# FFN's plain product with the weights stationary and all 512 tokens moving

## The chip, the cores and the metric

One core of a Trainium2 chip runs the whole program. The metric is the device time of one execution in microseconds. The engines are named as the profile names them: PE multiplies matrices (PEld loads its stationary operand), DVE and ACT are the vector and the scalar engine, POOL and SP issue most transfers.

## The reference

```python
def swiglu(x, w_in, w_out):
    gu = x @ w_in
    g, u = jnp.split(gu, 2, axis=-1)
    return (jax.nn.silu(g) * u) @ w_out
...
    for l in range(DEPTH):
        x = x + 0.5 * swiglu(rms_norm(x, ffn1_norm[l]), ffn1_w_in[l], ffn1_w_out[l])
        x = x + mixer(...)
        x = x + 0.5 * swiglu(rms_norm(x, ffn2_norm[l]), ffn2_w_in[l], ffn2_w_out[l])
    return rms_norm(x, final_norm)
```

There are 512 tokens of 1024 features, an inner width of 2816 and two layers, so four FFNs in all, all in float32. The change lies in the FFNs alone.

## The kernel before, in words

Every float32 product is made of three passes over halves of the operands: high times high, high times low, low times high. ACT writes the high half of a weight granule (`whi`, L201), DVE the low one (`wlo`, L208), out of `raw` granules of 512 KB that SP loads and to some of which POOL adds a second granule in flight. `ws.next()` hands out the next granule with two more already split; `raw` has nine buffers, `whi` and `wlo` three each.

An FFN (`stage_ffn`) first makes the 256 gate and the 256 up columns that are left over from its recursive scheme: this is the plain product `cl`. The other 5 × 512 columns follow in blocks `jb` = 0 to 4, each of seven products of Strassen's kind, called A, B, C in the trace. PSUM has eight banks of 128 × 512: the plain product holds four of them, A two, B two, and C, where it occurs, two more.

The input of the FFN lies transposed, features on the partitions: `xh` and `xl` are its high and low halves, in quarters of 4 × 128 features by 256 tokens. The first FFN gets them from a transposed copy of x. For the three later ones the last one or two quarters are transposed on PE while the plain product is already running (`norm.settle`, L670).

Before, a plain matmul has 128 tokens stationary and the 512 columns of the weights (256 gate, 256 up) moving, so the result has the tokens on its partitions. `plain(kt, w, kk, js)` does one feature tile `kt` for token halves `js`; features 4 to 7 are done for token half 1 first and then for half 0. `plain_out` applies 1/rms, which in this layout is one number per partition (`norm.r`, 128 × 4), in Silu's scale on ACT (L739) and in a multiply on DVE (L741). The outcome `th` must have the features on its partitions for the output product, so `late_at` and `to_at` (L643) send it through PE: eight 128 × 128 transposes for each FFN, and ACT copies the result to `at` (L647).

Engines run their own queues in order. DVE's and ACT's order is mostly that of a scheduler; PE's order follows the code.

Of the kernel before, what the change touches and what calls it, by code (L numbers as in the profile page):

```python
# [9 lines left out]
F32 = mybir.dt.float32  # L10
# [88 lines left out]
def encoder_kernel(  # L99
# [29 lines left out]
    def bank(s="ps"):  # L129
        return pp.tile([P, T], F32, tag="ps", name=nm(s))  # L130

    def pair(s="ps"):
        return [bank(s), bank(s)]
# [241 lines left out]
    def run(terms, again=False, late=False):  # L375

        if late:
            for ps, lh, ll, rh, rl, w, start, stop in terms:
                PE.matmul(ps, lh, rh, start=start, stop=False)
            for ps, lh, ll, rh, rl, w, start, stop in terms:  # L380
                PE.matmul(ps, ll, rh, start=False, stop=False)
            for ps, lh, ll, rh, rl, w, start, stop in terms:
                PE.matmul(ps, lh, rl, start=False, stop=stop)
            return
        for ps, lh, ll, rh, rl, w, start, stop in terms:
            PE.matmul(ps, lh, rh, start=start, stop=False, skip_group_check=again)  # L386
            PE.matmul(ps, *((lh, rl) if w == "l" else (ll, rh)), start=False, stop=False, skip_group_check=again)  # L387
        for ps, lh, ll, rh, rl, w, start, stop in terms:
            PE.matmul(ps, *((ll, rh) if w == "l" else (lh, rl)), start=False, stop=stop, skip_group_check=again)  # L389
# [227 lines left out]
    def snap(ps):  # L617
        t = slot(F32, "sn", (2, T))
        for b in range(2):
            S.activation(t[:, b, :], ps[b], AF.Copy)  # L620
        return t
# [5 lines left out]
    def stage_ffn(norm, nxt, late):  # L627
# [4 lines left out]
        def at_tile(h, j, c):  # L632
            if (h, j, c) not in at:
                at[h, j, c] = slot(F32, "at")
            return at[h, j, c]
# [14 lines left out]
                        S.activation(at_tile(h, j, c)[:, i, :], tr[:, k, :], AF.Copy)  # L650


        pcl = [pair("cl"), pair("cl")]

        def plain(kt, w, kk, js):
            wh, wl = w
            c = slice(kk * T, (kk + 1) * T)
            i, k = divmod(kt, 4)
            terms = []
            for j in js:  # L660
                for b in range(2):
                    t = slice((2 * j + b) * P, (2 * j + b + 1) * P)
                    terms.append((pcl[j][b], hx[i][:, k, t], lx[i][:, k, t], wh[:, c], wl[:, c], "r", kt == 0, kt == DT - 1))
            run(terms, late=not (norm.idx or kt))

        for g in range(2):
            w = ws.next()
            for kk in range(2):
                plain(2 * g + kk, w, kk, (0, 1))
            norm.settle()  # L670

        raw = norm.raw
        b11, b12, b21, b22 = raw[0, 0], raw[0, 1], raw[1, 0], raw[1, 1]

        w2 = [ws.next(), ws.next()]
        for js in ((1,), (0,)):
            for g in range(2):
                for kk in range(2):
                    plain(4 + 2 * g + kk, w2[g], kk, js)
        first = norm.idx == 0  # L680
        if not first:
            norm.rstd()
# [48 lines left out]
            5: t1, 6: t2, 7: t3,  # L731
        }
        late_at = []
        def plain_out():
            for j in range(2):
                th = slot(F32, "th", (2, 256))
                for b in range(2):
                    c = 2 * j + b
                    S.activation(th[:, b, :], pcl[j][b][:, 0:256], AF.Silu, scale=norm.r[:, c : c + 1])  # L739
                    u = pcl[j][b][:, 256:512]  # L740
                    V.scalar_tensor_tensor(th[:, b, :], u, norm.r[:, c : c + 1], th[:, b, :], ALU.mult, ALU.mult)  # L741
                late_at.append((th, j, 0, 2))

        if norm.idx:
            plain_out()

        def settle_at():
            while late_at:
                to_at(*late_at.pop(0))
# [73 lines left out]
        def pair_block(jb, late_at):  # L823

            one = jb in PAIRS
            pa = pair("A")
            product(pa, acts[1], K4, True)
            s1 = snap(pa)
            settle_at()
            if one:  # L830
                qa = kept["a"] = bank("qA")
                inner(qa, 1, True)
                V.tensor_tensor(s1[:, 0, :], qa, s1[:, 0, :], ALU.add)
            pb = pair("B")
            product(pb, acts[5], K4, True)
            sb = snap(pb)
            qa = kept["a"]
            if one:
                qb = bank("qB")
                inner(qb, 5, True)  # L840
                tb = kept["s"] = slot(F32, "sq", (2, T))[:, 0, :]
                S.activation(tb, qb, AF.Copy)
            else:
                tb = kept["s"]
                inner(qa, 7, False)
                V.tensor_tensor(tb, qa, tb, ALU.subtract)
                V.tensor_tensor(s1[:, 1, :], tb, s1[:, 1, :], ALU.subtract)
            settle_at()
            product(pa, acts[6], K4, False, again=True)
            s2 = snap(pa)  # L850
            if one:
                qc = bank("qC")
                inner(qc, 2, True)
                V.tensor_tensor(s1[:, 0, :], qc, s1[:, 0, :], ALU.subtract)
            else:
                inner(qa, 4, False)
                V.tensor_tensor(s1[:, 0, :], qa, s1[:, 0, :], ALU.subtract)
                z1 = gate(s1, 0)
            product(pa, acts[7], K4, False, again=True)
            less(pa, sb)  # L860
            if one:
                inner(qa, 6, False)
                V.tensor_tensor(s1[:, 1, :], qa, s1[:, 1, :], ALU.add)
            product(pb, acts[3], K4, False, again=True)
            less(pb, s2)
            z2 = gate(s2, 1)
            times(z2, [sb[:, 0, :], sb[:, 1, :]], 1)
            if one:
                inner(qb, 3, False)
                V.tensor_tensor(s1[:, 1, :], qb, s1[:, 1, :], ALU.subtract)  # L870
                z1 = gate(s1, 0)
            if jb == NB - 1:
                make(0)
                make(1)
            product(pa, acts[4], K4, False, again=True)
            times(z1, pa, 0)
            late_at += [(z2, 1, 2 + 4 * jb, 4), (z1, 0, 2 + 4 * jb, 4)]

        for jb in range(NB):
            f0 = 2 + 4 * jb  # L880
            if jb:
                if jb == 1:
                    inner_split()
                pair_block(jb, late_at)
                continue
            if first and jb == 0:
                with tc.manual_schedule(engines={mybir.EngineType.DVE, mybir.EngineType.Activation}):
                    pa = pair("A")
                    product(pa, acts[1], K4, True)
                    for j in range(2):  # L890
                        t = snap(pcl[j])
                        pcl[j] = [t[:, 0, :], t[:, 1, :]]
                    s1 = snap(pa)
                    second(s1)
                    pb = pair("B")
                    product(pb, acts[5], K4, True)
                    sb = snap(pb)
                    norm.squares(1, 1)
                    product(pa, acts[6], K4, False, again=True, ahead=1)
                    s2 = snap(pa)  # L900
                    for _ in norm.roots(0, 4):
                        pass
                    plain_out()
            else:
                pa, pb, s1, sb = two(jb)
                settle_at()
                product(pa, acts[6], K4, False, again=True)
                s2 = snap(pa)
            settle_at()
            if jb or not first:  # L910
                second(s1)
            z1 = gate(s1, 0)
            product(pa, acts[7], K4, False, again=True)
            less(pa, sb)
            product(pb, acts[3], K4, False, again=True)
            less(pb, s2)
            z2 = gate(s2, 1)
            times(z2, [sb[:, 0, :], sb[:, 1, :]], 1)
            if jb == NB - 1:
                make(0)  # L920
                make(1)
            product(pa, acts[4], K4, False, again=True)
            times(z1, pa, 0)
            late_at += [(z2, 1, f0, 4), (z1, 0, f0, 4)]
# [1220 lines left out]
```

## Time and profile before

| | |
|---|---|
| median of 3 runs | 1859.5 us (1858.61 to 1860.37) |
| profiled execution | 1858.22 us, span of its trace 1856.4 us |
| busy, of the span | PE 100%, PEld 85%, DVE 84%, ACT 65%, POOL 11% |
| chain that ended last | PE 99% |
| granted PE clock | 0.999 |
| transposes of FFN results (L643) | 352 in all, 32 of them for the plain products |

The span runs from the first to the last instruction of the trace; the 1.8 us beside it lie outside of it. A row of the timeline gives start, duration, engine, line, operation, result<-operands, shapes and count; for a matmul the moving operand comes first and the stationary one second. Ends of matmuls are modelled, their starts are recorded, so distances between starts are what counts on PE.

### The profile page before, as it was taken

Reading aid. Unit: us, or ns where it says so; the run is one execution under the profiler, and the core shown is the slowest. Engines: PE = TensorE matmul, PEld = TensorE weight load, DVE = VectorE, ACT = ScalarE, POOL = GpSimd, SP = SyncE. Lnnn points to the kernel's source line nnn. Section 1 sums busy time; section 2 is a strip of 40 time slices with the busy share of each in tenths; the row PEclk is TensorE's granted clock in tenths of the full one; section 3 lists DMA queues with packets and bytes.
Section 4 is the critical chain, followed back from the end, with each engine's and each line's share of the span. In section 5 each row is a group of like instructions: output and inputs, shape, how many; then the busy total and the mean of one; then the engine's idle time right before and its main releaser. Section 6 shows DMA issues by size and latency. Waiting matters only on the chain.

```text
span 1856.4 us, 26124 instructions
## 1 busy us (share of the span) xinstructions
PE 1847.7 (100%) x9564; PEld 1575.1 (85%) x9564; DVE 1556.3 (84%) x1915; ACT 1201.9 (65%) x1787; POOL 196.3 (11%) x235
## 2 busy tenths in 40 slices
PE   9999999999999999999999999999999999999998
PEld 7888888889998888888888888888899988888886
DVE  8888899758879787889978788997687797878898
ACT  6766666758656656666666666667676576656665
POOL 0011010100211011101001110110002100110010
PEclk9999999999999999999999999999999999999999
DMA  9788788774998479869757986987649984788695
GB/s 302 227 246 227 222 238 268 250 190 133 252 248 229 132 210 256 230 203 263 241 145 210 253 226 205 254 270 243 203 131 256 238 230 128 221 243 242 197 276 181
DMA packets 118385, 413.94 MB, mean 223 GB/s; under 512 B 13409, under 2 KB 13537, under 8 KB 118257
## 3 DMA queue, kind: packets, MB, share of 16 engines
q1 hardware_dynamic: 85712, 297.78, 45.6%
q0 software_dynamic: 32112, 113.71, 32.6%
q8 instruction: 75, 1.23, 0.3%
q10 hardware_dynamic: 432, 0.79, 0.1%
q14 instruction: 54, 0.43, 0.1%
HBM read 404.49 MB, written 6.29 MB: 221 GB/s over the span
## 4 chain that ended last, share of the span: by engine, by line
PE 99%; DVE 1%; issue 0%; ACT 0%; DVEq 0%; ACTq 0%
PE A L386 9%; PE A L389 9%; PE A L387 9%; PE o L386 7%; PE o L389 7%; PE o L387 7%; PE B L386 5%; PE B L387 5%; PE B L389 5%; PE ps L386 3%; PE ps L387 3%; PE ps L389 3%; PE tr L643 2%; PE cl L387 2%; PE cl L389 2%; PE cl L386 2%
## 5 line engine op out<-in xcount | busy, mean ns | idle before, releaser
L208 DVE TENSOR_TENSOR wlo<-raw,whi 128x1024 fp32r<-128x1024 f32 (+1 forms) x540 | 638.9, 1192 | 169.9 <-ACT whi L201 169.0
L201 ACT ACTIVATE whi<-raw 128x1024 fp32r<-128x1024 f32 (+1 forms) x540 | 555.1, 1033 | 318.8 <-PE A L387 89.7
L160 POOL DMA_DIRECT2D raw<-in_wst_dram x186 | 160.9, 869 | 1457.0 <-DMA raw<-in_wst_dram 755.9
L194 DVE TENSOR_TENSOR raw<-raw,raw 128x1024 f32<-128x1024 f32 (+1 forms) x144 | 171.3, 1194 | 2.7
L386 PE MATMUL A<-whi,xh 128*128 128x512 f32 x320 | 124.5, 389 | 0.0
L387 PE MATMUL A<-whi,xl 128*128 128x512 f32 x320 | 124.5, 389 | 0.0
L199 ACT ACTIVATE whi<-raw 128x1024 fp32r<-128x1024 f32 x84 | 87.2, 1038 | 42.1 <-issue 21.5
L206 DVE SCALAR_TENSOR_TENSOR wlo<-raw,whi 128x1024 fp32r<-128x1024 f32 x84 | 99.7, 1196 | 4.6 <-ACT whi L199 4.5
L389 PE MATMUL A<-wlo,xh 128*128 128x512 f32 x320 | 92.1, 389 | 0.0
L620 ACT ACTIVATE sn<-A 128x512 f32<-128x512 f32 x96 | 56.2, 591 | 46.4 <-PE A L389 46.3
L755 ACT ACTIVATE th<-sn,r 128x512 f32<-128x512 f32 x80 | 56.1, 715 | 46.2 <-DVE sn L625 42.5
L389 PEld LDWEIGHTS A<-wlo,xh 128*128 128x128 f32 x320 | 60.1, 188 | 12.5
L387 PEld LDWEIGHTS A<-whi,xl 128*128 128x128 f32 x320 | 60.1, 188 | 12.5
L386 PEld LDWEIGHTS A<-whi,xh 128*128 128x128 f32 x320 | 60.1, 188 | 12.4
L386 PE MATMUL B<-whi,t1h 128*128 128x512 f32 x160 | 63.0, 394 | 0.0
L386 PE MATMUL A<-whi,t2h 128*128 128x512 f32 x160 | 62.5, 391 | 0.0
L387 PE MATMUL B<-whi,xl 128*128 128x512 f32 x160 | 62.3, 390 | 0.0
L387 PE MATMUL B<-whi,t1l 128*128 128x512 f32 x160 | 62.3, 389 | 0.0
L387 PE MATMUL A<-whi,t2l 128*128 128x512 f32 x160 | 62.3, 389 | 0.0
L386 PE MATMUL A<-whi,t3h 128*128 128x512 f32 x160 | 62.3, 389 | 0.0
L387 PE MATMUL A<-whi,t3l 128*128 128x512 f32 x160 | 62.2, 389 | 0.0
L386 PE MATMUL B<-whi,xh 128*128 128x512 f32 x160 | 62.2, 389 | 0.0
(498 smaller groups left out, 4910.9 us busy)
## 6 DMA issues: line engine op xcount, KB each, us to landing
raw<-in_wst_dram SPq DMA_DIRECT2D x503, 512.0 KB
raw<-in_wst_dram POOLq DMA_DIRECT2D x200, 512.0 KB, 8.2
raw<-in_wst_dram SPq DMA_DIRECT2D x28, 256.0 KB
vc<-vd SPq DMA_DIRECT2D x28, 256.0 KB
bm<-in_near_dram SPq DMA_DIRECT2D x16, 384.0 KB
vd<-v SPq DMA_DIRECT2D x8, 512.0 KB
dft<-in_dft_dram POOLq DMA_DIRECT2D x4, 514.0 KB, 9.3
x<-in_xin_dram SPq DMA_DIRECT2D x4, 512.0 KB
```

Of the source, the lines that this page charges most:

```text
L160: z = G.dma_start(out=self.t, in_=wst[GRAN_AT[plus]][:, 0 : self.n], accum_op=ALU.add)
L194: V.tensor_tensor(self.raw.t, self.raw.t, self.add.t, ALU.add)
L199: S.activation(self.out[0][:, cs], self.raw.t[:, cs], AF.Copy, scale=-1.0)
L201: S.activation(self.out[0][:, cs], self.raw.t[:, cs], AF.Copy)
L206: self.last = V.scalar_tensor_tensor(lo, t, -1.0, hi.bitcast(F32), ALU.mult, ALU.subtract)
L208: self.last = V.tensor_tensor(lo, t, hi.bitcast(F32), ALU.subtract)
L386: PE.matmul(ps, lh, rh, start=start, stop=False, skip_group_check=again)
L387: PE.matmul(ps, *((lh, rl) if w == "l" else (ll, rh)), start=False, stop=False, skip_group_check=again)
L389: PE.matmul(ps, *((ll, rh) if w == "l" else (lh, rl)), start=False, stop=stop, skip_group_check=again)
L620: S.activation(t[:, b, :], ps[b], AF.Copy)
L643: PE.transpose(tr[:, k, b * P : (b + 1) * P], a[:, b, (q + k) * P : (q + k + 1) * P], ident)
L755: S.activation(th[:, b, :], g[:, b, :], AF.Silu, scale=norm.r[:, c : c + 1])
```

## The change

The plain product changes sides: 128 columns of the weights are stationary and all 512 tokens move. Banks `cl` 0 and 1 hold the gate features, 2 and 3 the up features, with features on the partitions. The count of matmuls stays (12 for each of 8 feature tiles). 1/rms now varies along the free dimension and has to be the same on all partitions: `spread_root` writes the 128 × 4 numbers to DRAM, four bytes apiece, and reads the 512 of them back to each of the 128 partitions (256 KB into `rr`), both on SP's queue. `plain_out` multiplies by `rr` on DVE, takes Silu on ACT and writes the product straight into `at`. It no longer stands right behind the plain product: in the three later FFNs it comes after the third product of block 0 (A, second time), in the first FFN in block 2.

```diff
-        pcl = [pair("cl"), pair("cl")]
-        def plain(kt, w, kk, js):
+        pcl = [bank("cl") for _ in range(4)]
+        def plain(kt, w, kk):
...
-            for j in js:
-                for b in range(2):
-                    t = slice((2 * j + b) * P, (2 * j + b + 1) * P)
-                    terms.append((pcl[j][b], hx[i][:, k, t], lx[i][:, k, t], wh[:, c], wl[:, c], "r", kt == 0, kt == DT - 1))
-            run(terms, late=not (norm.idx or kt))
+            mh, ml = hx[i][:, k, :], lx[i][:, k, :]
+            cs = [slice(kk * T + cb * P, kk * T + cb * P + P) for cb in range(4)]
+            if not norm.idx:
+                order = ((wh, mh), (wh, ml), (wl, mh))
+            else:
+                order = ((wh, mh), (wl, mh), (wh, ml))
...
+            for n, (lh, rh) in enumerate(order):
+                for cb in range(4):
+                    PE.matmul(
+                        pcl[cb], lh[:, cs[cb]], rh, start=first and n == 0 and len(order) == 3,
+                        stop=last and n == len(order) - 1,
+                    )
...
-        w2 = [ws.next(), ws.next()]
-        for js in ((1,), (0,)):
-            for g in range(2):
-                for kk in range(2):
-                    plain(4 + 2 * g + kk, w2[g], kk, js)
+        for g in range(2):
+            w = ws.next()
+            for kk in range(2):
+                plain(4 + 2 * g + kk, w, kk)
...
+        def spread_root():
+            rd = dp.tile([TB, P], F32, tag="rd", name=nm("rd"))
+            spread["r"] = t = slot(F32, "rr", (2, T))[:, 0, :]
+            nc.sync.dma_start(out=bass.AP(tensor=rd.tensor, offset=rd.offset, ap=[[1, P], [P, TB]]), in_=norm.r)
+            nc.sync.dma_start(out=t, in_=bass.AP(tensor=rd.tensor, offset=rd.offset, ap=[[0, P], [1, T]]))
...
-                    S.activation(th[:, b, :], pcl[j][b][:, 0:256], AF.Silu, scale=norm.r[:, c : c + 1])
-                    u = pcl[j][b][:, 256:512]
-                    V.scalar_tensor_tensor(th[:, b, :], u, norm.r[:, c : c + 1], th[:, b, :], ALU.mult, ALU.mult)
-                late_at.append((th, j, 0, 2))
+            r = spread.pop("r")
+            for f in range(2):
+                t = slot(F32, "th", (2, T))
+                V.tensor_tensor(t[:, 0, :], pcl[f], r, ALU.mult)
+                S.activation(t[:, 0, :], t[:, 0, :], AF.Silu)
+                V.tensor_tensor(t[:, 1, :], pcl[2 + f], r, ALU.mult)
+                for j in range(2):
+                    c = slice(j * 256, (j + 1) * 256)
+                    V.tensor_tensor(at_tile(0, j, 0)[:, f, :], t[:, 0, c], t[:, 1, c], ALU.mult)
         if norm.idx:
-            plain_out()
+            spread_root()
...
+            if first and jb == 2:
+                plain_out()
...
-            if jb or not first:
+            if not first:
+                plain_out()
                 second(s1)
```

In the first FFN ACT still copies the four banks to two tiles `sn` at once, before and after, so its banks come free early.

Three places of the built order follow. The first is PE in the second FFN of the first layer, block 0, where product B ends and the second use of A begins; before:

```order
2838 L389 MATMUL B_6197<-wlo_6177,t1h_6123 128x512 x2
2839 L643 MATMUL tr_6236<-ident,th_6145 128x128 x4
2840 L643 MATMUL tr_6243<-ident,th_6150 128x128 x4
2841 L386 MATMUL A_6155<-whi_6198,t2h_6133 128x512
2842 L387 MATMUL A_6155<-whi_6198,t2l_6134 128x512
```

and the same place in the changed kernel:

```order
2831 L387 MATMUL B_6185<-whi_6164,t1l_6118 128x512
2832 L389 MATMUL B_6185<-wlo_6165,t1h_6117 128x512 x2
2833 L386 MATMUL A_6143<-whi_6186,t2h_6127 128x512
2834 L387 MATMUL A_6143<-whi_6186,t2l_6128 128x512
2835 L386 MATMUL A_6143<-whi_6186,t2h_6127 128x512
```

The eight transposes are gone and A follows on B. The second place is DVE in the same block, around product C, in the changed kernel (`cl_5947` to `cl_5950` are the banks of the plain product in order, `C_6277` and `C_6278` those of C):

```order
677 L208 TENSOR_TENSOR wlo_6227<-raw_6015,whi_6226 128x1024
678 L208 TENSOR_TENSOR wlo_6245<-raw_6045,whi_6244 128x1024
679 L756 TENSOR_TENSOR th_6263<-cl_5947,rr_6140 128x512
680 L758 TENSOR_TENSOR th_6263<-cl_5949,rr_6140 128x512
681 L761 TENSOR_TENSOR at_6267<-th_6263 128x256
682 L761 TENSOR_TENSOR at_6269<-th_6263 128x256
683 L756 TENSOR_TENSOR th_6271<-cl_5948,rr_6140 128x512
684 L758 TENSOR_TENSOR th_6271<-cl_5950,rr_6140 128x512
685 L208 TENSOR_TENSOR wlo_6282<-raw_6075,whi_6281 128x1024
686 L761 TENSOR_TENSOR at_6267<-th_6271 128x256
687 L761 TENSOR_TENSOR at_6269<-th_6271 128x256
688 L208 TENSOR_TENSOR wlo_6300<-raw_6145,whi_6299 128x1024
```

Before, the rows 679 to 684, 686 and 687 are not here; four multiplies of 128 × 256 (L741) stand instead about ten rows earlier, next to the first granules of block 0. C's first bank is the one that row 679 reads and its second the one that row 680 reads. The third place is SP's queue at the beginning of the same FFN, in the changed kernel:

```order
205 L158 DMA raw_6145<-in_wst_dram 128x1024
206 L749 DMA rd_6139<-r_6107 128x4x1
207 L158 DMA raw_6203<-in_wst_dram 128x1024
208 L750 DMA rr_6140<-rd_6139 128x512
209 L158 DMA raw_6224<-in_wst_dram 128x1024
```

Rows 206 and 208 are new; the loads around them keep their order. Row 208 waits for row 206 to land, and the loads from row 209 on stand behind it.

More of the change, by code (lines that the diff above doesn't have):

```diff
@@ L650, in to_at @@
                         S.activation(at_tile(h, j, c)[:, i, :], tr[:, k, :], AF.Copy)
-        pcl = [pair("cl"), pair("cl")]
-        def plain(kt, w, kk, js):
+        pcl = [bank("cl") for _ in range(4)]
+        def plain(kt, w, kk):
             wh, wl = w
-            c = slice(kk * T, (kk + 1) * T)
             i, k = divmod(kt, 4)
-            terms = []
-            for j in js:
-                for b in range(2):
-                    t = slice((2 * j + b) * P, (2 * j + b + 1) * P)
-                    terms.append((pcl[j][b], hx[i][:, k, t], lx[i][:, k, t], wh[:, c], wl[:, c], "r", kt == 0, kt == DT - 1))
-            run(terms, late=not (norm.idx or kt))
+            mh, ml = hx[i][:, k, :], lx[i][:, k, :]
+            cs = [slice(kk * T + cb * P, kk * T + cb * P + P) for cb in range(4)]
+            first, last = kt == 0, kt == DT - 1
+            if not norm.idx:
+                order = ((wh, mh), (wh, ml), (wl, mh))
+            else:
+                order = ((wh, mh), (wl, mh), (wh, ml))
+            if kt and not norm.idx:
+                for cb in range(4):
+                    PE.matmul(pcl[cb], wh[:, cs[cb]], mh, start=False, stop=False)
+                    PE.matmul(pcl[cb], wh[:, cs[cb]], ml, start=False, stop=False)
+                order = order[2:]
+            for n, (lh, rh) in enumerate(order):
+                for cb in range(4):
+                    PE.matmul(
+                        pcl[cb], lh[:, cs[cb]], rh, start=first and n == 0 and len(order) == 3,
+                        stop=last and n == len(order) - 1,
+                    )
         for g in range(2):
@@ L668, in stage_ffn @@
             for kk in range(2):
-                plain(2 * g + kk, w, kk, (0, 1))
+                plain(2 * g + kk, w, kk)
             norm.settle()
@@ L733, in stage_ffn @@
         late_at = []
-        def plain_out():
[L735 to L739, printed above, removed]
-                    u = pcl[j][b][:, 256:512]
-                    V.scalar_tensor_tensor(th[:, b, :], u, norm.r[:, c : c + 1], th[:, b, :], ALU.mult, ALU.mult)
-                late_at.append((th, j, 0, 2))
+        spread = {}
+        def spread_root():
[3 more added lines that the diff above has]
+            nc.sync.dma_start(out=t, in_=bass.AP(tensor=rd.tensor, offset=rd.offset, ap=[[0, P], [1, T]]))
+        def plain_out():
+            r = spread.pop("r")
[7 more added lines that the diff above has]
+                    V.tensor_tensor(at_tile(0, j, 0)[:, f, :], t[:, 0, c], t[:, 1, c], ALU.mult)
         if norm.idx:
-            plain_out()
+            spread_root()
         def settle_at():
@@ L890, in stage_ffn @@
                     for j in range(2):
-                        t = snap(pcl[j])
-                        pcl[j] = [t[:, 0, :], t[:, 1, :]]
+                        t = snap(pcl[2 * j : 2 * j + 2])
+                        pcl[2 * j : 2 * j + 2] = [t[:, 0, :], t[:, 1, :]]
                     s1 = snap(pa)
@@ L902, in stage_ffn @@
                         pass
-                    plain_out()
+                spread_root()
             else:
```

## The prediction

> **What bounds the kernel now.** I read the page first, then the waits of PE, then the timelines of PE, DVE and ACT around the four plain products. The page:
>
> ```profile
> span 1856.4 us, 26124 instructions
> PE 1847.7 (100%) x9564; PEld 1575.1 (85%) x9564; DVE 1556.3 (84%) x1915; ACT 1201.9 (65%) x1787; POOL 196.3 (11%) x235
> ...
> PE 99%; DVE 1%; issue 0%; ACT 0%; DVEq 0%; ACTq 0%
> ```
>
> PE has hardly a hole and is 99% of the chain that ended last. So an instruction taken off PE is worth its place in PE's queue, and work on DVE, ACT and the transfers costs nothing until PE waits for it. The list of waits of PE's weight loads (engine, line, releaser: us in total, times, longest) shows how little it waits:
>
> ```profile
> PEld L146 <- issue: 2.8, 10, 0.3
> ...
> PEld cl L387 <- DVE xl L394: 0.7, 2, 0.4
> PEld cl L379 <- ACT whi L201: 0.5, 1, 0.5
> PEld tr L643 <- DVE th L741: 0.3, 1, 0.3
> PEld cl L389 <- DVE wlo L208: 0.2, 1, 0.2
> ```
>
> What stands in the first row is the warm-up at the start. Behind it the only waits near the change are two for `xl` at the entry of a plain product and one for `th` at the transposes. There is almost nothing to win by waiting less; the question is what the transposes cost and whether a new wait appears.
>
> **The change part by part.** *Transposes off PE.* The tile view gives the length of one, the timeline their spacing:
>
> ```profile
> L643 PE MATMUL tr<-ident,th x352: 270/272/332, 60.6 to 1748.0; 128*128 128x128 f32 x176
> ```
>
> ```profile
> 634.45 0.62 PE L389 MATMUL B<-wlo,t1h 128*128 128x512 f32 x2
> 634.91 1.03 PE L643 MATMUL tr<-ident,th 128*128 128x128 f32 x8
> 635.70 0.48 PE L386 MATMUL A<-whi,t2h 128*128 128x512 f32 x1
> 636.01 0.39 PE L387 MATMUL A<-whi,t2l 128*128 128x512 f32 x1
> ```
>
> ```profile
> 60.40 0.39 PE L386 MATMUL B<-whi,xh 128*128 128x512 f32 x1
> ...
> 60.73 0.47 PE L387 MATMUL B<-whi,xl 128*128 128x512 f32 x1
> ...
> 61.52 0.48 PE L389 MATMUL B<-wlo,xh 128*128 128x512 f32 x1
> ...
> 62.14 0.47 PE L389 MATMUL B<-wlo,xh 128*128 128x512 f32 x1
> 62.46 0.40 PE L386 MATMUL A<-whi,xh 128*128 128x512 f32 x1
> ```
>
> ```profile
> 641.25 0.39 PE L386 MATMUL C<-whi,xh 128*128 128x512 f32 x1
> ...
> 642.16 0.39 PE L386 MATMUL C<-whi,xh 128*128 128x512 f32 x1
> ```
>
> In plain running four starts take 642.16 − 641.25 = 0.91 us, 0.2275 us each. In a later FFN eight transposes hold the queue for 635.70 − 634.91 = 0.79 us, and the matmul behind them is followed after 0.31 instead of 0.23 us: 0.79 + 0.08, with the hundredth at the front, 0.88 us. I take this for all three later FFNs: 2.64 us. In the first FFN the eight are strewn between matmuls: from 60.40 to 62.46 there are four matmul starts, so 2.06 − 4 × 0.2275 = 1.15 us for the transposes (the wait of 0.3 us for `th` is in it). Sum: −3.79 us. Each lies on the path alone, nothing runs on PE beside it.
>
> The Trainium skill, "TensorE: Matmul & The Clock Gate", Part 4 on the PE-mode transpose, says that a transpose took about 275 ns in one kernel; the trace agrees on the length of one, 272 ns, but starts them 0.10 us apart. By the page's figure the sum would be 32 × 0.275 = 8.8 us, an estimate that nothing below rests on.
>
> *The plain matmuls.* Their number and shape stay: 96 for each FFN, 128 × 128 stationary and 512 moving. Before as after each has its own weight load. Cost zero; bounds ± 0.3 us, since a group of four has the same spacing of 0.23 us in both orders (the rows of C alternate two passes into one bank, the pairs of L389 go on to the next).
>
> *Entry of a plain product.* All 512 tokens are now needed by the first matmul of a feature tile. In the second FFN of layer one:
>
> ```profile
> 599.03 1.06 ACT L393 ACTIVATE xh<-xr 128x1024 fp32r<-128x1024 f32 x1
> ...
> 611.33 1.10 ACT L393 ACTIVATE xh<-xr 128x1024 fp32r<-128x1024 f32 x1
> ```
>
> ```profile
> 600.21 0.39 PE L386 MATMUL cl<-whi,xh 128*128 128x512 f32 x1
> ...
> 601.11 0.39 PE L386 MATMUL cl<-whi,xh 128*128 128x512 f32 x1
> 601.45 0.50 PE L387 MATMUL cl<-whi,xl 128*128 128x512 f32 x1
> 601.78 0.40 PE L386 MATMUL cl<-whi,xh 128*128 128x512 f32 x1
> ...
> 613.14 0.39 PE L386 MATMUL cl<-whi,xh 128*128 128x512 f32 x1
> ```
>
> ```profile
> 604.88 0.17 DVE L535 SCALAR_TENSOR_TENSOR r<-rt,r 128x4 f32<-128x4 f32 x1
> ...
> 613.02 1.22 DVE L394 TENSOR_TENSOR xl<-xr,xh 128x1024 fp32r<-128x1024 f32 x1
> ```
>
> Before, PE lost 0.34 + 0.33 − 2 × 0.2275 = 0.21 us at 601.11 and 601.45, waiting for `xl`; that is one of the two waits of the list. Now `xl` is asked for eight matmuls in, 1.8 us later, and this wait goes. What is late next is `xh`: it ends at 600.09 and its weight load would like to start a matmul earlier than 600.21, at 599.98, so some 0.1 us come back. Twice −0.1, so −0.2 us in all (bounds −0.4 and +0.2).
>
> Features 4 to 7 lose the head start that token half 0 had: before, its turn came 24 matmuls after 613.14. Now its quarter is wanted at 613.14, as `xh` at once and as `xl` 8 × 0.2275 = 1.82 us later, at 614.96. `xh` ends at 612.43, `xl` at 614.24: 0.7 us to spare for each, so nothing. The order of ACT and DVE up to there is the same. Were that cover gone, each us would cost one.
>
> *Banks held longer.* In the later FFNs the four banks now wait for rows 679 to 684 of DVE's order, and C's two need the first two of these. Durations, DVE on 128 × 512 and 128 × 256, the last weights before C, ACT's table load and Silu:
>
> ```profile
> 638.92 1.23 DVE L208 TENSOR_TENSOR wlo<-raw,whi 128x1024 fp32r<-128x1024 f32 x1 [1.66 <-ACT whi L201]
> ...
> 645.53 0.69 DVE L625 TENSOR_TENSOR sn<-C,sn 128x512 f32<-128x512 f32 x1
> ```
>
> ```profile
> 617.56 0.42 DVE L689 TENSOR_TENSOR v<-xr 128x256 f32<-128x256 f32 x1
> ```
>
> ```profile
> 640.09 0.60 ACT L620 ACTIVATE sn<-A 128x512 f32<-128x512 f32 x1 [1.21 <-PE A L389]
> ```
>
> ```profile
> 624.85 1.28 ACT L739 ACT_TABLE_LOAD   x1
> ```
>
> ```profile
> L755 ACT ACTIVATE th<-sn,r x80: 704/716/725, 63.2 to 1738.7; 128x512 f32<-128x512 f32 x80
> ```
>
> On the clock of before, row 678 ends at 640.15, row 679 at 640.84 and row 680 at 641.53. C's first load starts at 641.25 − 0.23 = 641.02, that of its second bank at 642.16 − 0.23 = 641.93. Both are met, by 0.2 and 0.4 us: cost zero, bounds 0 and 3 × 0.5 us. Then DVE stands at row 681 until ACT is through: copy of A to 640.69, table 1.28, Silu 0.72, so 642.69. Rows 681 to 684 take 2 × 0.42 + 2 × 0.69 = 2.22 us, to 644.91, and `wlo_6282`, queued behind, ends at 646.14. A's next product starts 24 × 0.2275 = 5.46 us after C, at 646.71, and wants it eight matmuls on, at 648.5. The new DVE work is 4 × 0.69 + 4 × 0.42 = 4.4 us for each FFN, and it is hidden; ACT gets lighter, two Silus for four and no copies.
>
> *Block 2 of the first FFN* is the tightest:
>
> ```profile
> 119.47 1.22 DVE L208 TENSOR_TENSOR wlo<-raw,whi 128x1024 fp32r<-128x1024 f32 x1 [2.85 <-ACT whi L201]
> ...
> 124.39 1.22 DVE L208 TENSOR_TENSOR wlo<-raw,whi 128x1024 fp32r<-128x1024 f32 x1
> ```
>
> ```profile
> 129.47 0.62 PE L389 MATMUL qA<-wlo,vh 128*128 128x512 f32 x2
> ```
>
> The `wlo` of 124.39 serves the matmul at 129.47. In the new order there stand between the row at 119.47 and it four multiplies (0.69), two products (0.42), and, as before, an add (1.22), a `wlo` (1.22) and two combinations (0.69). Whole durations give 119.47 + 1.22 + 2.76 + 0.84 + 2.44 + 1.38 = 128.11 for its start and 129.33 for its end; PE's load is due at 129.24. Rows that follow directly overlap by some 0.08 us, so I take zero; bounds 0 and 0.5 us, once.
>
> *The two transfers.* r is ready at 605.05. SP issues rows 206 and 208 then, and what stands behind them is the next load of weights. The list of waits of SP's queue from 605 to 640:
>
> ```profile
> SPq L158 <- DVE raw L194: 23.0, 2, 19.5
> ```
>
> SP would stand still there for 19.5 us anyway, until DVE frees a buffer, so a wait for the first transfer to land delays no load. No row shows a transfer of 4-byte pieces. The longest mean landing of the page is
>
> ```profile
> at<-at POOLq DMA_DIRECT2D x2, 512.0 KB, 12.3
> ```
>
> Twice that is 24.6 us as the upper end, zero the lower one. I take the upper one: `rr` is there by 629.7, and row 679 wants it at 640.15. Cost zero.
>
> Sum: −3.79 − 0.2 = −4.0, and 0.1 us for the margins of 0.2 us that I have read too kindly: −3.9 us. The profiled execution took 1858.2 us, of which 1.8 lie outside the span, and would come to 1854.3. The median of the runs shown is 1.3 us above it, and I keep that distance: **1855.6 us**, 0.21% less than before.
>
> **The rivals.** *A new wait eats the gain.* The margins at C (0.2 us in three FFNs), in block 2 and at the entries are small, and a plain product that waits on `xh` for half a microsecond more, or a C that waits 0.3 to 1 us for its bank, takes back 0.3 to 3.5 us of 3.9: 1856 to 1859 us. For it: the margins come from one execution. Against it: PE and the engines that feed it move together, and DVE idles in this stretch.
>
> *Slower: `rr` is late.* DVE takes its queue in order, so at row 679 a missing `rr` holds all weights behind it, and PE with them, a microsecond for each, in three FFNs. That begins when the two transfers together take more than 640.15 − 605.05 = 35.1 us, and it makes the kernel slower by over 3.7 us from 35.1 + (3.9 + 3.7) / 3 = 37.6 us on. At 40 us it would be 1855.6 + 3 × 4.9 = 1870 us. Against it: 24.6 us is the upper end above.
>
> *The transposes cost their length.* If taking them out freed 272 ns each, the gain would be 32 × 0.272 = 8.7 us, with the entries 8.8, and the time 1850.7 us. Against it: the spacing in the rows of 634.91 and 635.70. The page named above would have it so.
>
> *The change does not do what it says* is out: the built order has the matmuls and lacks the transposes.
>
> **How the numbers follow.** Forecast 0.65, a new wait 0.20, `rr` late 0.12, the whole length 0.03. A measurement of this kernel can tell about 0.2%, 3.7 us, from no change. The forecast of −3.9 lies just beyond it; with its own spread of about 0.5 us some two thirds of its chance, 0.44, are faster and 0.21 the same. With the 0.03 faster is 0.47; with the eaten gain the same is 0.41; slower 0.12. The range runs from 1854.0, where the entries give all and the runs fall as the lowest of before did, to 1860.4, where the whole gain is eaten and they fall as the highest did; it leaves out the last two rivals.
>
> **What would show it.** In the profile after: 320 transposes of L643 instead of 352; B's last matmul and A's first 0.23 us apart; no wait of PE for `cl`, C or A above 0.3 us. C waiting for the DVE multiplies of `cl`, or qA for `wlo` in block 2, would show the first rival; DVE idle before its first multiply with `rr`, released by a DMA, the second. A gain over 5 us or a loss would make the prediction wrong.

## The result and the profile after

| | before | after |
|---|---|---|
| median of 11 runs each | 1859.5 us (1858.6 to 1860.37) | 1855.52 us (1854.67 to 1857.63) |
| ratio | | 0.9979, 95% interval 0.9970 to 0.9987 |
| profiled execution | 1858.22 us, span 1856.4 | 1855.69 us, span 1853.9 |
| transposes of FFN results | 352 | 320 |
| granted PE clock | 0.999 | 0.999 |

The kernel became 4.0 us faster, 0.2%, and the interval of the ratio lies below 1; 3.9 had been forecast. The page of the changed kernel shows the same picture, PE without holes and nearly the whole chain; DVE has 16 instructions more, ACT 16 fewer:

```profile
span 1853.9 us, 26082 instructions
PE 1844.5 (99%) x9532; PEld 1571.2 (85%) x9532; DVE 1563.9 (84%) x1931; ACT 1196.6 (65%) x1771; POOL 196.4 (11%) x235
...
PE 98%; DVE 1%; DMA 0%; issue 0%; ACT 0%; ACTq 0%; DVEq 0%
```

The place where B ends and the second use of A begins, in the second FFN, stood before with eight transposes between 634.91 and 635.70. Here is the timeline of PE after, and the tile view of the transposes that remain:

```profile
633.59 0.62 PE L389 MATMUL B<-wlo,t1h 128*128 128x512 f32 x2
634.05 0.39 PE L386 MATMUL A<-whi,t2h 128*128 128x512 f32 x1
634.27 0.39 PE L387 MATMUL A<-whi,t2l 128*128 128x512 f32 x1
```

```profile
L643 PE MATMUL tr<-ident,th x320: 270/272/273, 72.5 to 1744.3; 128*128 128x128 f32 x160
```

The last two matmuls of B, and A right behind them, run at the pace of plain running: 634.05 − 633.59 = 0.46 us for two. The waits of PE's weight loads after (engine, line, releaser: us, times, longest):

```profile
PEld o L389 <- DVE wlo L208: 1.2, 2, 0.7
PEld cl L668 <- DVE xl L396: 0.7, 1, 0.7
PEld cl L672 <- ACT whi L201: 0.7, 1, 0.7
PEld o L386 <- ACT whi L201: 0.6, 1, 0.6
PEld A L386 <- ACT sn L620: 0.6, 2, 0.4
PEld cl L672 <- ACT xh L393: 0.4, 2, 0.2
```

No wait for C and none for `qA`: the banks and block 2 kept their margins. The waits for `xl` at the later entries are gone, and `xh` is asked for instead, 0.2 us each. New beside the list of before are A's wait for ACT's copy `sn` and those of the last output product `o` for weights. The two waits of 0.7 us for `cl` lie in the first FFN's plain product, where the kernel before waited 0.5 us for `whi`; in its second trace, below, it waited 0.7 us for `xl` there and 1.4 for `whi`.

PE runs without holes, so the start of one and the same matmul in both traces tells where the lead comes from:

| matmul | start before | start after | lead |
|---|---|---|---|
| first FFN, block 0, second use of B | 55.87 | 56.21 | −0.34 |
| first FFN, A with `xh` behind it | 62.46 | 61.65 | 0.81 |
| second FFN, first A | 624.02 | 623.17 | 0.85 |
| second FFN, A with `t2h` | 635.70 | 634.05 | 1.65 |
| second FFN, C | 641.25 | 639.49 | 1.76 |
| third FFN, C | 968.75 | 966.09 | 2.66 |
| fourth FFN, C | 1563.85 | 1560.19 | 3.66 |
| last output product, its first matmul | 1742.28 | 1738.63 | 3.65 |
| last output product, its last matmul | 1848.54 | 1846.30 | 2.24 |

The first FFN's transposes gave 0.81 + 0.34 = 1.15 us, those of the second 1.65 − 0.85 = 0.80 us, and 0.11 more up to C by the pace of the product behind them. The third and the fourth give 0.91 us each likewise, from their own first A to their C (the first A leads there by 1.75 and 2.76 us). Against this stand 0.3 us lost in block 0 of the first FFN and 1.4 us in the last product. The experiments ask whether the transposes alone explain the gain, what the spread of 1/rms costs, and what these two losses are.

### The profile page after: what moved, and what is told of

Same layout as the page of the kernel before. It is cut to its first block, busy times and chain, and to the rows that moved or that the text cites. A ratio compares the mean times of both kernels' runs of the same rounds, so it can differ in the third digit from the quotient of the medians.

```text
span 1853.9 us, 26082 instructions
## 1 busy us (share of the span) xinstructions
PE 1844.5 (99%) x9532; PEld 1571.2 (85%) x9532; DVE 1563.9 (84%) x1931; ACT 1196.6 (65%) x1771; POOL 196.4 (11%) x235
## 4 chain that ended last, share of the span: by engine, by line
PE 98%; DVE 1%; DMA 0%; issue 0%; ACT 0%; ACTq 0%; DVEq 0%
PE A L386 10%; PE A L389 9%; PE A L387 9%; PE o L387 7%; PE o L386 7%; PE o L389 7%; PE B L386 5%; PE B L387 5%; PE B L389 5%; PE cl L672 4%; PE ps L386 3%; PE ps L387 3%; PE ps L389 3%; PE tr L643 2%; PE tr L471 1%; PE C L389 1%
```

## The experiments

Each time stands beside that of the kernel before on the same chip (1859.25 to 1859.44 us).

**Transposes put back.** Into the changed kernel, behind the product C of block 0 (in the first FFN behind the second A), with n = 8 and n = 40:

```diff
+        def idle_transposes(n):
+            tr = bank("tr")
+            for q in range(n):
+                PE.transpose(tr[:, q % 4 * P : q % 4 * P + P], ident, ident)
...
                 second(s1)
+            idle_transposes(n)
```

> The changed kernel with eight transposes of the identity put back on PE in block 0 of every FFN, 32 in all; nobody reads their result. Theory of the queue place: each costs what separates two starts, 0.10 to 0.11 us, so 32 x 0.11 = 3.5 us more than the changed kernel: about 1859.0 us, the time before. Rival, the whole length: 32 x 0.272 = 8.7 us more, 1864.2 us. Rival, the gain comes from the swapped sides or the lighter ACT and not from the transposes: no change, 1855.5 us.

> The same with forty instead of eight for each FFN, 160 in all, for a difference well above the scatter. Queue place: 160 x 0.104 to 0.11 = 16.6 to 17.6 us above the changed kernel, 1872.1 to 1873.1 us. Whole length: 160 x 0.272 = 43.5 us, 1899 us. Swapped sides: 1855.5 us.

Measured: 1858.51 us with 8 (ratio to before 0.9996, 0.9987 to 1.0005) and 1873.05 us with 40 (1.0070, 1.0058 to 1.0083). The timeline of PE with 8, in the second FFN:

```profile
644.81 0.62 PE L389 MATMUL C<-wlo,xh 128*128 128x512 f32 x2
645.27 1.03 PE L769 MATMUL tr<-ident 128*128 128x128 f32 x8
646.06 0.48 PE L386 MATMUL A<-whi,t3h 128*128 128x512 f32 x1
646.37 0.39 PE L387 MATMUL A<-whi,t3l 128*128 128x512 f32 x1
```

Again 0.79 us for eight, and 0.31 instead of 0.23 us behind them. From 8 to 40 the time grows by 14.54 us for 128 transposes, 0.114 us each; the spacing forecast holds, and the length of 272 ns does not. Put back, the 32 bring the changed kernel to the time of before within the interval. They cost 2.2 to 3.0 us over the changed kernel's two medians, where 3.5 had been expected. In the trace they cost 0.91 us in each later FFN and 0.60 in the first, where the eight cover a part of the wait for `sn`, of which below; that makes 3.3 us. The medians lie 0.3 to 1.1 us below that; this stays open, and the two medians of the changed kernel are themselves 0.8 us apart.

**The kernel before without the transposes.** ACT's copy takes `th` as it stands, so that these columns of the result stay untransposed:

```diff
             for q in range(0, n, 2):
+                if not f0:
+                    S.activation(at_tile(0, j, 0)[:, 0:2, :], a, AF.Copy)
+                    continue
```

> The kernel before without the 32 transposes of the plain products; ACT copies th to at as it stands, so these columns are left untransposed. Sides, Silu, scale and order stay as before. Queue place: 1.15 + 3 x 0.88 = 3.8 us less than before, 1855.7 us, all of the gain of the change. Whole length: 8.7 us less, 1850.8 us. Swapped sides: no change, 1859.5 us.

Measured: 1855.53 us, ratio 0.9977 (0.9968 to 0.9986). The changed kernel took 1855.52 us in its first series and, as the next run shows, 1856.32 us on this chip. In the trace the last product starts at 1738.59 us, in that of the changed kernel at 1738.63. Sides, Silus and scale as before, transposes gone: the whole gain, as near as the times tell. The swapped sides are worth nothing by themselves that shows here; they are what makes the transposes needless.

**The changed kernel again.**

> The changed kernel a second time, for a second trace of it. 1855.5 us. In its first trace PE lost 0.34 us more than before at the entry of the first FFN, and 1.4 us in the last output product, where weights came late. If these belong to the change, they stand here again, at the same products, within 0.3 us; if they are chance in the arrival of transfers, they are gone or elsewhere.

Measured: 1856.32 us, ratio 0.9984 (0.9975 to 0.9993), 2.9 us under the kernel before on its chip. PE's wait for `sn` in the first FFN stands at the same matmul (its start is at 50.63 us here, 50.58 in the first trace). That of the last product is there too, at other matmuls, and the product took 107.50 us from its first to its last start, 107.67 in the first trace.

**The kernel before again.**

> The kernel before, for a second trace of it. Its first trace had no wait in the last output product, 106.26 us long, while ten traces of the changed kernel and its relatives had 106.5 to 108.7 us there. Chance in the arrival of weights: this trace has some wait there too, 106.5 us or more. A price of PE's lead: 106.3 us again.

Measured: 1859.56 us in one run. The waits of PE's weight loads in its last product:

```profile
PEld o L389 <- DVE wlo L208: 1.1, 2, 0.6
PEld o L386 <- ACT whi L201: 0.4, 1, 0.4
```

107.47 us for the product from its first to its last start, where the first trace had 106.26. So a wait there comes without the change too. Over 14 traces of all kernels here this product took 106.3 to 108.7 us, while the three other output products took 108.05, 108.95 and 108.05 us with hardly an exception. The trace of before that the prediction worked from was a good one, 1.3 us under its median.

This second trace also bears on the table above. From the second use of A to the second use of B in block 0 of the first FFN PE takes 10.91 us in both traces of before and 11.22 and 11.26 in those of the changed kernel, so the 0.3 us lost there are the change's. But the last product starts at 1742.67 us here: against this trace the lead is 4.04 us, not 3.65. Of the difference 0.24 us arise in front of block 0's second A. Sums of leads from one pair of traces are good to some 0.4 us.

**Multiplying early.** The three later FFNs have the multiplies and Silus right behind the plain product:

```diff
         if norm.idx:
             spread_root()
+            plain_out()
...
             if not first:
-                plain_out()
                 second(s1)
```

> In the three later FFNs the multiplies with rr and their Silus stand as early as the code of before had them, right behind the plain product, instead of behind the third product of block 0. DVE then reaches the first of them at about 622.3 us of the changed kernel's trace, and the second transfer is issued at 612.4. Theory (the transfers are early and DVE has 2.1 us idle there): no change, 1855.5 to 1856.3 us, PE without new waits. Rival (the place is what hides the transfer): DVE stands until rr has landed, and with a landing of 12 us or more PE waits 2 us or more in each of the three FFNs: 1862 us or more.

Measured: 1856.73 us, ratio 0.9985 (0.9977 to 0.9994), the same as the changed kernel within its interval. DVE's timeline and SP's queue in the second FFN:

```profile
622.66 0.69 DVE L756 TENSOR_TENSOR th<-cl,rr 128x512 f32<-128x512 f32 x1 [0.37 <-PE cl L672]
```

```profile
604.30 0.38 SPq L749 DMA_DIRECT2D rd<-r  x1
607.53 0.33 SPq L158 DMA_DIRECT2D raw<-in_wst_dram  x1
613.34 0.33 SPq L750 DMA_DIRECT2D rr<-rd  x1
626.99 0.33 SPq L158 DMA_DIRECT2D raw<-in_wst_dram  x1
```

Here, and in the fourth FFN, the first multiply waits for PE and not for `rr`, which has landed at most 9.3 us after its issue. In the third FFN DVE does stand for `rr`, issued at 941.59:

```profile
950.36 0.69 DVE L756 TENSOR_TENSOR th<-cl,rr 128x512 f32<-128x512 f32 x1 [2.40 <-DMA rr<-rd]
```

That is a landing of 8.8 us. PE lost nothing by it: its C starts at 966.06 us, in the changed kernel at 966.09. So the early place costs nothing that the times show, but in the third FFN it leaves no cover on DVE; there the later place does hide the end of the second transfer.

**A longer way for 1/rms.** One or two steps more in DRAM, in the later FFNs, k = 2 and k = 1:

```diff
+            for _ in range(k if norm.idx else 0):
+                old, rd = rd, dp.tile([TB, P], F32, tag="rd", name=nm("rd"), bufs=k + 1)
+                nc.sync.dma_start(out=bass.AP(...rd, ap=[[1, P], [P, TB]]), in_=bass.AP(...old, ap=[[1, P], [P, TB]]))
             nc.sync.dma_start(out=t, in_=bass.AP(tensor=rd.tensor, offset=rd.offset, ap=[[0, P], [1, T]]))
```

> The numbers of 1/rms take two more DRAM to DRAM steps, four bytes apiece, before they are spread, all on SP's queue, in the three later FFNs. Each step is taken at 8.0 us, as the first transfer showed. The last transfer is then issued at 604.3 + 3 x 8.05 = 628.5 instead of 612.4 us, SP's next load about 2 us later than before, and DVE wants rr at 638.3. Theory (25 us of cover): no change, 1855.5 to 1856.3 us. Rival (SP's loads or rr have no cover of that size): 3 x several us, 1865 us or more.

> One more DRAM to DRAM step ahead of the spread instead of two. With two, the steps took 8.7, 12 and 8.9 us, rr was issued at 634.2 us and landed 6.2 us later, 2 us after DVE wanted it, and C's product waited in all three later FFNs. With one it should be issued at about 625 us and land at 631, 7 us ahead of DVE. Theory (rr costs only from the point where it lands behind DVE's row): no wait at C, 1855.5 to 1856.3 us. Rival (each further step costs transfers or SP time of its own): some 6 us, half of what two steps cost, 1862 us.

Measured: with two steps 1871.73 us, ratio 1.0061 (1.0049 to 1.0074), with one 1855.95 us, ratio 0.9982 (0.9973 to 0.9991). For two steps the stated theory fell. SP's queue and DVE's timeline in the second FFN, then in the third:

```profile
604.29 0.38 SPq L749 DMA_DIRECT2D rd<-r  x1
612.99 0.65 SPq L752 DMA_DIRECT2D rd<-rd  x1
...
625.27 0.58 SPq L752 DMA_DIRECT2D rd<-rd  x1
634.17 0.34 SPq L756 DMA_DIRECT2D rr<-rd  x1
```

```profile
640.36 0.69 DVE L762 TENSOR_TENSOR th<-cl,rr 128x512 f32<-128x512 f32 x1 [2.02 <-DMA rr<-rd]
```

```profile
972.78 0.69 DVE L762 TENSOR_TENSOR th<-cl,rr 128x512 f32<-128x512 f32 x1 [6.01 <-DMA rr<-rd]
```

From issue to issue the steps took 8.7, 12.3 and 8.9 us, more than the 8.05 of the estimate, and the last transfer 640.36 − 634.17 = 6.2 us. In the second FFN DVE was held 2.0 us and PE's C 1.75, in the third 6.0 and 5.7, in the fourth 1.9 and 1.65: PE pays a microsecond for each that `rr` is late, less about a quarter of one. In the third FFN 3.0 us more came behind the pause, of which the last section tells. The trace is of the fastest of the five executions, 1867.26 us; what the others lost beyond it, no trace shows. With one step `rr` was issued at 627.33 and nothing waited for it. SP's next loads came 7.6 us late with two steps (634.61 for 627.01) and no product waited for weights behind them. In the changed kernel `rr` is issued at 612.41, so there by 618.6 if it takes 6.2 us, and wanted at 638.30: 19.7 us to spare. The third FFN is tighter: issued at 942.18 and wanted at 964.89, with the landing of 8.8 us seen above it has 13.9 us to spare.

**Half the tokens at a time.** Each plain matmul of the changed kernel in two:

```diff
-                    PE.matmul(pcl[cb], lh[:, cs[cb]], rh, ...)
+                    for z in (slice(0, 256), slice(256, 512)):
+                        PE.matmul(pcl[cb][:, z], lh[:, cs[cb]], rh[:, z], ...)
```

> Each plain matmul of the changed kernel in two, 256 tokens moving in each: the same columns, twice the instructions and weight loads. In the mixer of the changed kernel's trace matmuls with 256 moving start 0.120 us apart, those with 512 start 0.2267 us apart. Theory of the starts: 4 x 96 x (2 x 0.120 - 0.2267) = 5.1 us more, 1860.7 us, and the gain of the change is gone. Rival, columns alone count: 1855.5 us. Rival, the weight loads of 0.165 us each set the pace: 4 x 96 x (2 x 0.165 - 0.2267) = 39.7 us more, 1895 us.

Measured: 1860.44 us, ratio to before 1.0006 (0.9997 to 1.0015). PE's timeline in the second FFN:

```profile
602.30 1.12 PE L674 MATMUL cl<-xl,whi 128*128 128x256 f32 x8
603.26 1.00 PE L674 MATMUL cl<-xh,whi 128*128 128x256 f32 x7
```

Eight starts in 0.96 us, 0.120 each, as in the mixer. The same columns in twice the instructions cost 4.1 to 4.9 us over the changed kernel's two medians, all that the transposes had given. The swap pays only as long as all 512 tokens move at once.

**The first FFN's copy of A.** In both traces of the changed kernel PE loses 0.3 us where A is used the third time; PE's and ACT's timelines, from the first of them:

```profile
49.98 0.61 PE L389 MATMUL A<-wlo,t2h 128*128 128x512 f32 x2
50.58 0.50 PE L386 MATMUL A<-whi,t3h 128*128 128x512 f32 x1
50.91 0.40 PE L387 MATMUL A<-whi,t3l 128*128 128x512 f32 x1
```

```profile
48.04 2.00 ACT L201 ACTIVATE whi<-raw 128x1024 fp32r<-128x1024 f32 x2
49.93 0.59 ACT L620 ACTIVATE sn<-A 128x512 f32<-128x512 f32 x1
```

The scheduler has put two `whi` ahead of the copy; before, it was one, and the copy ran at 49.24. The edit moves two sums of squares out of ACT's way:

```diff
                     second(s1)
+                    norm.squares(1, 1)
                     pb = pair("B")
...
-                    norm.squares(1, 1)
                     product(pa, acts[6], K4, False, again=True, ahead=1)
```

> In both traces of the changed kernel PE waits in block 0 of the first FFN, at 50.2 us, for ACT's copy of A: 0.31 us that the kernel before did not lose. ACT had run its rows without idle time since 44.9 us. Here its two last sums of squares (1.2 us) stand a product earlier, where ACT idles. Theory: the copy is in time and PE's wait at A is gone, 0.3 us, 1855.2 us or no difference that the times can tell; the trace decides. Rival (the order of the copy behind the next weights is the cause, not ACT's lateness): the wait of 0.3 us stays.

Measured: 1856.10 us, ratio 0.9985 (0.9976 to 0.9994). The wait for `sn` is gone from this place, as the theory had it, but a shorter one stands at the next copy, 51.70 us: from the second use of A to that of B PE takes 11.08 us, between the 10.91 of before and the 11.22 of the changed kernel. So about half of the 0.3 us came back. And the profiled execution, 1858.97 us and the longest of its eleven, has a new wait between its starts at 76.08 and 78.99 us, for ACT's copy of the next transposes, which stands behind a late weight:

```profile
PEld B L386 <- ACT at L647: 2.9, 1, 2.9
```

**The spread in the first FFN.** Why that weight was late is the question of the last pair. The second transfer goes to the beginning of block 1, first alone, then together with the edit above:

```diff
-                spread_root()
+                spread_out()
...
                 if jb == 1:
                     inner_split()
+                if first and jb == 1:
+                    spread_back()
```

> In the first FFN alone the second transfer is issued at the start of block 1, behind two more loads of weights, instead of right behind the first. In six of eight traces with the spread ACT waited 0.3 to 5.4 us for weights between 69 and 77 us, in the two without it never; transfers fell there from 265 to 56 GB/s (62 to 66 us). Theory (SP stands for 8 us with loads behind it): the loads flow on, over 150 GB/s in that stretch, and ACT's waits for transfers there are gone; the time stays 1855.5 to 1856.3 us, since PE rarely waited. Rival (the pieces of four bytes themselves hold the transfers up): under 100 GB/s and ACT's waits as before.

> Both repairs of the first FFN: the second transfer late, and the two sums of squares a product earlier, which alone took PE's 0.3 us wait at A away but met a late load at 76 us (2.7 us). Theory: neither wait stands in the trace, block 0's B starts at about 55.9 us and the rest keeps that lead: 0.3 us under the changed kernel, 1855.2 us. Rival (the late load has nothing to do with SP's wait): a wait for weights of over 1 us at 70 to 80 us again.

Measured: 1855.76 us, ratio 0.9981 (0.9973 to 0.9990), and 1856.70 us, ratio 0.9985 (0.9976 to 0.9994). The stretch from 62 to 66 us, by the windows (busy time of PE, PEld, DVE, ACT, POOL, then granted clock, DMA share and GB/s), in before, in after, with the late second transfer, and with both edits:

```profile
62.00:66.00 4.00, 4.00 (x21) 3.36 (x20) 3.02 (x5) 4.00 (x8) 0.72 (x1) 1.00 1.03 265
```

```profile
62.00:66.00 4.00, 4.00 (x20) 3.30 (x19) 4.00 (x5) 3.51 (x4) 0.00 (x0) 1.00 0.50 56
```

```profile
62.00:66.00 4.00, 4.00 (x19) 3.30 (x18) 4.00 (x6) 3.34 (x4) 0.00 (x0) 1.00 1.38 170
```

```profile
62.00:66.00 4.00, 4.00 (x19) 3.32 (x18) 4.00 (x6) 3.32 (x4) 0.00 (x0) 1.00 0.37 28
```

Two or three loads now went out behind the first transfer, at 57.3 to 60.6 us, where before two had gone out, at 57.99 and 60.23; then SP stood 7.8 and 4.8 us at the second transfer, where before it had stood for a free buffer. The transfers still fell. With the late second transfer alone the 170 GB/s are above the 150 that the theory had named, but the hole is only four microseconds later: 53 GB/s from 66 to 70 us, 248 before. And the three loads that POOL issues on a queue of its own between 56 and 61 us landed late too: after 6.8 to 11.8 us before, 11.6 to 15.5 in after, 11.5 to 16.8 and 15.1 to 19.7 with the edits. ACT waited 2.4 us for weights in the one and 4.6 and 2.2 in the other. With both edits B started at 56.12 us, not at the expected 55.9, and PE waited again:

```profile
PEld B L386 <- ACT at L647: 2.1, 1, 2.1
```

So SP's standing queue is not the cause, and the rival holds as far as it goes: the hole comes with the first transfer, the one of four-byte pieces, and it holds up another queue's loads as well. In all 11 traces with the spread the stretch ran at 28 to 171 GB/s, in the three without it at 265 to 277. No run sends the same 2 KB in larger pieces; that their size is the cause, and how they hold the others up, is not shown. No version built on the changed kernel beat it.

## Why the prediction was right

*What bounds the kernel* and *transposes off PE*: right, and the reason is shown from both sides. Taking 32 transposes out of the kernel before gives the changed kernel's time, putting them back gives that of before. The first FFN's term was 1.15 us and is 1.15; those of the others were 0.88 and are 0.91. The page "TensorE: Matmul & The Clock Gate" of the Trainium skill, Part 4, gives about 275 ns for a transpose; 0.114 us for each of 128 more is what one costs in this queue. The rival that charged the length is refuted.

*Plain matmuls at zero*: right, the third FFN's plain product takes 22.44 us from its first to its last start in both kernels. This holds only for 512 moving tokens; with 256 the starts are 0.120 us apart and not half of 0.2267.

*Entry*: −0.2 forecast. From the start of the plain product to the first A behind it the second and the fourth FFN take 0.16 and 0.12 us less and the third shows nothing, −0.28 in all, with `xh` late in the place of `xl`, as argued.

*Banks and block 2*: the first multiply with `cl` was placed at 640.15 on the clock of before, 638.4 less the lead, and started at 638.30; C did not wait, nor did `qA`.

*The two transfers*: the size was off and the conclusion right. 24.6 us had been allowed; in the second FFN the first took 8.05 us and the second 6.2, in the third 10.3 and, by the trace with the early multiplies, 8.8. The rival with a late `rr` is a real mechanism at the right place: DVE wants it 638.30 − 604.3 = 34.0 us after the first issue, where 35.1 had been worked out, and with 36.1 us (604.29 to 640.36) PE paid 1.75. Its price of a microsecond for each was right for small delays and too low for the long one in the third FFN, by 3.0 us. The change stays 19.7 us short of that point in the second FFN and, by the estimate above, 13.9 in the third.

*What the prediction missed.* The step on ACT's and DVE's order spoke of the later FFNs and of block 2, not of the first FFN's block 0, where ACT's order changed by one row and 0.3 us were lost. It was covered by the 0.1 us allowed for such margins only in part, and the sign that no wait for `cl`, C or A is above 0.3 us failed for A (0.4 us on its weight load) and, in the first FFN, for `cl`. And the step on the transfers looked only at SP's queue in the second FFN, where SP stands anyway, and not at what the spread does to the other transfers. In the later FFNs they slow down beside it too, from 224 to 137 GB/s between 604 and 612 us in the second, and no product waits for them. In the first FFN the spread takes some 0.8 MB out of a stretch of 4 us ((265 − 56) GB/s × 4 us). ACT's slack bore that in the changed kernel's two traces. In three of the eleven traces with the spread it became a wait of PE of 1.6 to 2.7 us: both with the moved squares, and the one with one step more, whose code in the first FFN is that of the changed kernel; there the first transfer took 16.9 us from its issue to that of the second, in the changed kernel's first trace 9.8. The first rival, a new wait, is thus real, at a place the prediction had not named, and small.

That the forecast met the median within 0.1 us is partly luck. By the two first traces the lead up to the last product is 3.65 us, 0.25 short of 3.9: 0.34 lost up to block 0's second B, 0.13 in the mixers and 0.04 behind the C's, against 0.08 more from the transposes, 0.08 more at the entries and the margin of 0.1. With the second trace of before it is 4.04. The medians say 4.0, with an interval from 2.4 to 5.6 us, and 2.9 in the second series.

## What to carry to other kernels

Where the chain is the matmul engine alone, price an instruction on it by the distance between starts at its very place, not by its length, and check the next product's pace too: eight transposes cost 0.79 us and 0.1 more behind them. Choosing the sides of a product so that its result comes out the way the next one wants it was worth its transposes here with 512 moving; with 256 the gain was gone. Work that goes off the critical engine lands elsewhere: look at each of its places in the program, not only at the one that repeats most, for what else is busy there, the transfers above all.

## What the runs showed of the hardware

A transfer of 2 KB in pieces of four bytes took 8 to 13 us in the second FFN, from its issue to the issue that waited for it, and in the first FFN the weights' transfers fell beside it from 265 to 277 GB/s to 28 to 171. "DMA: Bandwidth & Descriptors" of the Trainium skill, Specifications, asks for pieces of 512 bytes and more for the full rate; the runs agree in direction, and none here has the same transfer in larger pieces.

When `rr` was 6 us late, PE paid more than the wait. Its timeline in the third FFN with two steps, and the windows (granted clock third from the right):

```profile
967.42 0.61 PE L389 MATMUL A<-wlo,t2h 128*128 128x512 f32 x2
973.62 0.77 PE L386 MATMUL C<-whi,xh 128*128 128x512 f32 x1 [5.58 <-DVE th L762]
974.18 0.63 PE L387 MATMUL C<-whi,xl 128*128 128x512 f32 x1
974.61 0.63 PE L386 MATMUL C<-whi,xh 128*128 128x512 f32 x1
...
980.70 0.39 PE L386 MATMUL C<-whi,xh 128*128 128x512 f32 x1
980.92 0.39 PE L387 MATMUL C<-whi,xl 128*128 128x512 f32 x1
```

```profile
966.00:968.00 2.00, 2.00 (x10) 1.34 (x8) 0.77 (x1) 1.26 (x2) 0.00 (x0) 1.00 0.00 0
974.00:979.00 5.00, 5.00 (x13) 3.84 (x13) 3.16 (x6) 3.11 (x5) 0.00 (x0) 0.50 0.72 261
```

For 6 us behind the pause the granted clock was 0.50 and starts were 0.43 us apart, which cost 3.0 us on top of 5.7. The pauses of 1.7 us in the other two FFNs left the clock alone. "TensorE: Matmul & The Clock Gate" of the Trainium skill, Part 1, has the clock halve after an idle window of about 3.4 us, and this agrees. A late `rr` is therefore dearer than a microsecond for each from some delay on, which lies here between the 2.0 and the 6.0 us that DVE waited.
